# Forget-gate logits: moved from fp32 matmuls at the start to VectorE multiply-and-sum tasks spread over the middle

## The chip, the cores and the metric

The kernel runs on one core of one Trainium2 chip. The metric is the device time of one execution in microseconds (us). Five engines work side by side, each with its own instruction queue in program order: TensorE (PE in the profile, with PEld for its weight loads), VectorE (DVE), ScalarE (ACT), GpSimd (POOL) and SyncE (SP, which here only issues DMAs).

## The reference, cut to what matters

One layer of a gated hybrid encoder, 512 tokens by 2048 channels, all float32. Everything is projected from the normalised input; four columns of that projection are the forget logits, one for each head of branch A:

```python
hn = rmsnorm(x, norm_g)                                  # (1, 512, 2048)
proj = jnp.einsum('bsd,dc->bsc', hn, w_in)               # 6144 + 4 + 6144 columns
f_logit = proj[..., QKVG_COLS:QKVG_COLS + N_HEADS] + b_f # the 4 forget columns
...
log_f = jax.nn.log_sigmoid(f_logit)                      # in forgetting_attention (branch A)
c = jnp.cumsum(log_f, axis=1)
logits = logits + c[:, :, lo:hi, None] - c[:, :, None, :hi]
```

Branch A is attention with this cumulated bias; branch B is attention over a band with a learned bias; branch C is stick-breaking attention. Each branch output is gated, projected up, weighted by merge gates, summed, projected once more and added to x.

The forget logit of a token is therefore rstd[token] times the dot product of its 2048 inputs with w_f * norm_g, for each of four heads, plus b_f.

## The kernel before, in words

**The matmuls.** Weights arrive in float32 tiles of 128 x 1024 (`raw`, eight buffers). ACT rounds each to a high part (`wh`, line 375, three buffers), DVE subtracts to get the low part (`wl`, line 383, two buffers), and PE makes three products of the halves (all through the helper of line 265). One such tile is a *unit*; a list `units` gives the order. The first 9 units are the projection of head 0 of branch C, with x read, scaled and split at the same time; the next 8 are the first block of merge gates; then come 11 stretches of 28 units, each a Strassen product (seven products of half size) that gives one more head and one more block of gates. After them follow the up projections and the output projection. POOL issues DMAs that add a second weight tile onto the first for some Strassen products.

**The order.** A planner (`Flow`) runs when the kernel is built. Every piece of work is a generator that yields what it needs: an event, a number of buffers (`Slots`), or an engine with an estimated duration. The planner takes the piece that can start first on its engine and, among equals, the one that is due first (its ready time plus its `slack`); the instructions are written out in this order, and each engine keeps to it. `fetch` issues a load on SP's queue and estimates its landing. The function `at(u, g, slack)` starts the piece `g` when PE begins unit `u`.

**Buffers.** `t2s` stands for 20 tiles of 128 x 512 float32 in SBUF, shared by all attention work; pieces with a slack over 1 must leave one free. `atts` stands for 4 PSUM banks for attention, `accs` for the 4 banks of the units.

**The forget logits before.** x is kept transposed (channels on partitions). While the first head is projected, `quad(..., early=True)` puts, after the units that end at k tile 11 and 15, eight float32 matmuls each: the 128 x 4 slice `wf` of the constants is stationary, the scaled x tile (`xraw`) streams with 512 columns, and `tile_position` places four of them side by side in the array, so that `first_ps` gets four partial sums. Only then (`f_used`) may `combos` overwrite those x tiles with the sums that Strassen needs. `take_f` copies the bank out and stores it to DRAM; `norm_x` stores rstd to DRAM with one element for each descriptor; `forget_bias` (from unit 17 on) loads both back in another layout, with heads on groups of 32 partitions and 16 tokens in a row, adds the four partial sums, multiplies with rstd, makes the log-sigmoid with small instructions and stores it in `fd2`. The first reader is the softmax of head 0 of branch A (`soft_start`, which broadcasts a row of `fd2` and cumulates it), in the eighth Strassen stretch.

Of the kernel before, what the change touches and what calls it, by code (L numbers as in the profile page):

```python
# [15 lines left out]
P = 128  # L16
# [147 lines left out]
def hybrid_kernel(  # L164
# [2 lines left out]
    xT: bass.AP,  # L167
    xn: bass.AP,
    consts: bass.AP,
    w_col: bass.AP,  # L170
    b_gate: bass.AP,
    rel: bass.AP,
# [36 lines left out]
    def att():  # L209
        return pt.tile([P, S], F32, tag="att", name=nm("att"))  # L210
# [84 lines left out]
    gn = small_in[:, 0:KT]  # L295
    gqk = small_in[:, KT:KT + 4]
    bfc = small_in[:, KT + 4:KT + 5]
    wf = small_in[:, KT + 5:].rearrange("p (k h) -> p k h", h=NH)

    oneb = cp.tile([P, P], BF16, name="oneb")  # L300
    nc.vector.memset(oneb, 1.0)
# [112 lines left out]

    raw_hi = [Event() for _ in range(KT)]
    raw_ev = [Event() for _ in range(KT)]
    scaled, f_used = [Event() for _ in range(KT)], [Event() for _ in range(KT)]
    used_g = [Event() for _ in range(UK)]
    x1 = [Parts("x1", [raw_ev[k], Event()]) for k in range(UK)]
    x2 = [Parts("x2", [raw_ev[k + UK]] * 2) for k in range(UK)]  # L420
# [1 line left out]
    t23 = [None] * UK  # L422
    t4 = [None] * (UK // 2)
    xraw, x_in = [None] * KT, [Event() for _ in range(KT)]
    first_ps = att()
    atts.free.pop()
    nc.vector.memset(first_ps, 0.0)
    early_ps = att()
    for _ in range(WARM):
        nc.tensor.matmul(early_ps[:, :P], oneb, oneb, start=True, stop=True)  # L430
# [49 lines left out]
        yield DVE, dve_us(size)  # L480
        nc.vector.scalar_tensor_tensor(y, w, 1.5, t, op0=ALU.add, op1=ALU.mult)

    rd = dp.tile([QB, P], F32, name="rd")

    def norm_x():

        for i in range(NQ * QB):
            yield n_in[i]
            yield ACT, 0.75, 12.0 + 1.5 * i
            x = xnat[i // 2][:, i % 2, :]  # L490
            nc.scalar.activation(x, x, AF.Square, accum_out=ssq[:, i // NQ, i % NQ:i % NQ + 1])
        give(xps, UK)
        small_n = cp.tile([P, 4, QB], F32, name="small_n")
        m, tmp = small_n[:, 0, :], [small_n[:, i, :] for i in range(1, 4)]
        yield DVE, 0.2
        nc.vector.tensor_reduce(m, ssq, axis=AX.X, op=ALU.add)
        yield from rsqrt(rstd, m, D, tmp, QB)
        set_(rstd_ev)
        nc.sync.dma_start(rd.rearrange("b p -> p b"), rstd)

    def combos(k):

        due = (70.0 + 3 * k,)
        late = (80.0 + 3 * k,)
        for kt in (k, k + UK):
            yield raw_ev[kt]
            yield f_used[kt]
        a, b = xraw[k], xraw[k + UK]
        q = dve_us(HS)
        yield (DVE, q, *due)  # L510
        nc.vector.tensor_sub(a[:, LH], a[:, LH], a[:, RH])
        yield (DVE, q, *due)
        nc.vector.tensor_sub(a[:, RH], b[:, RH], a[:, RH])
        yield (DVE, q, *due)
        minus(b[:, RH], b[:, RH], a[:, LH])
        yield (DVE, q, *due)
        minus(b[:, LH], b[:, RH], b[:, LH])
        yield xps, 1
        t23[k] = Parts("t23")
# [187 lines left out]

    gl = {}
    yd = {}
    f_ev, f2_ev = Event(), Event()  # L710
    fd, fd2 = dp.tile([4, NH, S], F32, name="fd"), dp.tile([NH, S], F32, name="fd2")

    def forget_bias():

        T = S // 32
        lf = cp.tile([P, 5 * T], F32, name="lf")
        v, u, s, p, r = (lf[:, i * T:(i + 1) * T] for i in range(5))
        yield f_ev
        yield rstd_ev
        nc.sync.dma_start(lf[:, :4 * T].rearrange("p (g t) -> p g t", g=4), fd.rearrange("g h (c t) -> (h c) g t", t=T))  # L720
        for h in range(NH):
            nc.sync.dma_start(r[32 * h:32 * (h + 1), :], rd.rearrange("b (c t) -> (b c) t", t=T))
        yield Event(f_ev.t + 8.0)
        q = 0.15
        yield DVE, 4 * q
        nc.vector.tensor_add(v, v, u)
        nc.vector.tensor_add(s, s, p)
        nc.vector.tensor_add(v, v, s)
        nc.vector.tensor_mul(v, v, r)
        yield DVE, 2 * q  # L730
        nc.vector.tensor_scalar(v, v, bfc, 0.0, op0=ALU.add, op1=ALU.add)
        nc.vector.scalar_tensor_tensor(u, v, -1.0, v, op0=ALU.mult, op1=ALU.min)
        yield ACT, q
        nc.scalar.activation(u, u, AF.Exp)

        yield DVE, 5 * q
        nc.vector.tensor_scalar_add(s, u, 2.0)
        nc.vector.reciprocal(s, s)
        nc.vector.tensor_mul(s, s, u)
        nc.vector.tensor_mul(u, s, s)  # L740
        nc.vector.tensor_scalar_mul(p, u, 1.0 / 17.0)
        for k in range(7, 0, -1):
            yield DVE, q
            nc.vector.scalar_tensor_tensor(p, p, 1.0 / (2 * k + 1), u, op0=ALU.add, op1=ALU.mult)
        yield DVE, 4 * q
        nc.vector.scalar_tensor_tensor(p, p, 1.0, s, op0=ALU.add, op1=ALU.mult)
        nc.vector.tensor_scalar_mul(p, p, 2.0)
        nc.vector.tensor_scalar(v, v, -1.0, 0.0, op0=ALU.mult, op1=ALU.max)
        nc.vector.tensor_add(v, v, p)
        nc.sync.dma_start(fd2.rearrange("h (c t) -> (h c) t", t=T), v)  # L750
        f2_ev.t = flow.fin + 3.0
# [340 lines left out]
    def quad(parts, g, done, early=False):  # L1092
# [8 lines left out]
        def mms(kts):  # L1101
            def go(u):
                first, last = kts[0] == 0, kts[-1] == KT - 1
                if not early or last:
                    bank = (accs, acc) if first else None
                    yield from products(u, ps, kts, tbs, block, first, last, bank, done=lambda tb: done(tb, ps[tb]),
                                        outer=first or last)
                    if not early:
                        for kt in kts:
                            if kt < UK:  # L1110
                                set_(used_g[kt])
                else:
# [12 lines left out]
                if early and kts[-1] in (11, 15):  # L1125
                    b = kts[-1] - 3
                    eight = [*range(b - UK, b - UK + 4), *range(b, b + 4)]
                    for kt in eight:
                        yield scaled[kt]
                    yield PE, 2.2  # L1130
                    for kt in eight:
                        j = kt % 4
                        nc.tensor.matmul(first_ps[32 * j:32 * j + NH, :], wf[:, kt, :], xraw[kt],  # L1133
                                         start=kt < 4, stop=kt >= KT - 4, tile_position=(0, 32 * j))
                    for kt in eight:
                        set_(f_used[kt])
            return go

        def src(kts):
# [5 lines left out]
    def take_f():  # L1145
        yield t2s, 1
        yield ACT, act_us(S)
        v = t2("f")
        nc.scalar.activation(v, first_ps, AF.Copy)
        give(atts)  # L1150
        for j in range(4):
            nc.sync.dma_start(fd[j], v[32 * j:32 * j + NH, :])
        stored(t2s, 1, 16)
        f_ev.t = flow.fin + 3.0

    def first_head():
        hd = Head(C, 0)
# [7 lines left out]
        units[-1].after = take_f  # L1165
        u0 = len(units)
        at(u0 - 2, lambda: brow(0))

# [4 lines left out]
            give(accs)  # L1173

        units.extend(quad([[k, k + 1] for k in range(0, KT, 2)], gate_group(0), gates_done))
        at(u0 + OFF["fb"], forget_bias)
        for d, g in hd.stages():
            at(u0 + 1 + 2 * d // 3, g)

# [283 lines left out]
NX = 28  # L1463
NR = 8

OFF = dict(cs=4, ct=12, co=14, s=8, t=14, o=16, s1=3, t1=4, o1=5, fb=8)

_OUT = (QB, NQ, P, S)

# [45 lines left out]
```

## Time and profile before

| what | value |
|---|---|
| median of 3 runs | 1312.24 us (1312.24 to 1312.25) |
| profiled execution | 1312.22 us, of which 1310.5 us span |
| PE busy | 1305.2 us |
| DVE, ACT, POOL busy | 1026.3, 755.6, 91.3 us |
| moved by DMA | 266.03 MB, mean 203 GB/s |
| TensorE clock granted | 1.000 |

The span runs from the first to the last instruction; the execution's time has 1.7 us more around it. The profile groups instructions by line, engine and tile names, gives for each engine what ended its idle times, and follows the chain of work that ended last back to the start. The weight loads (PEld) have measured starts, which makes their distance a good clock for the pace of PE; the ends of matmuls are modelled.

### The profile page before, as it was taken

The page shows a single profiled execution, that of the slowest core. Times are in us where ns is not written, and L with a number is a line of the kernel's source. Part 1 is how long each engine was busy: PE and PEld are TensorE (multiplying, and loading weights), DVE is VectorE, ACT ScalarE, POOL GpSimd, SP SyncE. Part 2 cuts the span into 40 slices and gives each one's busy share as a digit, 9 for nine tenths or more (in the row PEclk, how much of TensorE's full clock was granted, in tenths as well). Part 3 has the DMA queues.
Part 4 walks back from the last instruction along what each step waited for, and adds up shares of the span by engine and source line. Part 5 has one row for each costly group of instructions (what it writes and reads, how often), then busy time and mean ns, then how long its engine had stood idle before and what let it go on. Part 6 is the DMA issues. An engine that isn't in the chain of part 4 may idle for free.

```text
span 1310.5 us, 17137 instructions
## 1 busy us (share of the span) xinstructions
PE 1305.2 (100%) x6028; PEld 1079.2 (82%) x6028; DVE 1026.3 (78%) x1422; ACT 755.6 (58%) x1270; POOL 91.3 (7%) x115
## 2 busy tenths in 40 slices
PE   9999999999999999999999999999999999999998
PEld 7788888888888888888888888888888888888887
DVE  6877796897968768687687886877879668798767
ACT  7655465564556646566475764666668555463442
POOL 0000001100111001101011000110100000000110
PEclk9999999999999999999999999999999999999999
DMA  9755677766777768777687776866786756638983
GB/s 357 223 139 146 179 208 197 220 186 184 209 187 225 199 170 231 173 226 201 179 233 166 211 208 179 248 150 203 215 257 212 273 179 198 181 89 258 253 240 129
DMA packets 89063, 266.03 MB, mean 203 GB/s; under 512 B 11264, under 2 KB 11264, under 8 KB 88976
## 3 DMA queue, kind: packets, MB, share of 16 engines
q1 hardware_dynamic: 71552, 205.94, 46.8%
q0 software_dynamic: 14976, 54.53, 23.3%
q10 hardware_dynamic: 2448, 4.46, 0.9%
q8 instruction: 47, 0.77, 0.3%
q14 instruction: 40, 0.33, 0.1%
HBM read 245.19 MB, written 19.70 MB: 202 GB/s over the span
## 4 chain that ended last, share of the span: by engine, by line
PE 99%; DMA 1%; SPq 0%; ACT 0%; DVE 0%; issue 0%
PE acc L265 92%; PE att L816 1%; PE att L941 1%; PE att L1031 1%; PE att L1030 1%; PE att L261 1%; PE att L262 1%; PE att L260 1%; PE att L1029 1%; PE att L1300 1%; DMA raw<-in_w_col 1%; PE att L1133 0%; SPq L277 0%; PE att L913 0%; ACT wh L375 0%; DVE s L703 0%
## 5 line engine op out<-in xcount | busy, mean ns | idle before, releaser
L375 ACT ACTIVATE wh<-raw 128x1024 fp32r<-128x1024 f32 (+1 forms) x404 | 426.5, 1056 | 389.6 <-PE acc L265 326.7
L383 DVE TENSOR_TENSOR wl<-raw,wh 128x1024 fp32r<-128x1024 f32 (+1 forms) x405 | 493.0, 1219 | 195.1 <-PE acc L265 139.8
L265 PE MATMUL acc<-wh,x 128*128 128x512 f32 x1664 | 434.3, 393 | 0.2
L265 PEld LDWEIGHTS acc<-wh,x 128*128 128x128 f32 x1664 | 307.9, 188 | 64.5 <-ACT wh L375 1.0
L265 PE MATMUL acc<-wh,t 128*128 128x512 f32 x1056 | 271.3, 390 | 0.0
L265 PE MATMUL acc<-wl,x 128*128 128x512 f32 x832 | 231.5, 392 | 0.0
L265 PEld LDWEIGHTS acc<-wh,t 128*128 128x128 f32 x1056 | 197.5, 188 | 40.3
L265 PEld LDWEIGHTS acc<-wl,x 128*128 128x128 f32 x832 | 155.2, 188 | 32.2
L265 PE MATMUL acc<-wl,t 128*128 128x512 f32 x528 | 147.9, 391 | 0.0
L281 POOL DMA_DIRECT2D raw<-in_w_col x88 | 76.1, 864 | 879.0 <-ACT wh L375 143.9
L589 DVE TENSOR_TENSOR raw<-raw,raw 128x1024 f32<-128x1024 f32 x104 | 126.6, 1218 | 0.1
L265 PEld LDWEIGHTS acc<-wl,t 128*128 128x128 f32 x528 | 98.4, 188 | 20.1
L265 PE MATMUL acc<-wh,m 128*128 128x512 f32 x448 | 112.9, 389 | 0.0
L265 PE MATMUL acc<-wh,y 128*128 128x512 f32 x384 | 103.1, 390 | 0.0
L265 PEld LDWEIGHTS acc<-wh,m 128*128 128x128 f32 x448 | 84.1, 188 | 17.4
L265 PEld LDWEIGHTS acc<-wh,y 128*128 128x128 f32 x384 | 71.9, 188 | 15.0
L265 PE MATMUL acc<-wl,m 128*128 128x512 f32 x224 | 62.5, 390 | 0.0
L265 PE MATMUL acc<-wl,y 128*128 128x512 f32 x192 | 59.4, 391 | 0.0
L265 PEld LDWEIGHTS acc<-wl,m 128*128 128x128 f32 x224 | 41.9, 188 | 8.8 <-DVE wl L383 0.2
L265 PEld LDWEIGHTS acc<-wl,y 128*128 128x128 f32 x192 | 35.8, 188 | 7.1
L246 ACT ACTIVATE ah<-att 128x512 fp32r<-128x512 f32 (+3 forms) x48 | 20.9, 436 | 30.3 <-PE att L941 30.3
L1266 DVE TENSOR_TENSOR sg<-acc,sg 128x512 f32<-128x512 f32 x48 | 32.8, 689 | 5.0 <-PE acc L265 2.6
(176 smaller groups left out, 1083.9 us busy)
## 6 DMA issues: line engine op xcount, KB each, us to landing
raw<-in_w_col SPq DMA_DIRECT2D x235, 512.0 KB, 4.7
raw<-in_w_col POOLq DMA_DIRECT2D x88, 512.0 KB, 8.2
raw<-in_w_out SPq DMA_DIRECT2D x40, 512.0 KB, 4.7
raw<-in_w_up SPq DMA_DIRECT2D x24, 512.0 KB, 3.8
sg<-gl SPq DMA_DIRECT2D x48, 256.0 KB, 4.7
raw<-in_w_out POOLq DMA_DIRECT2D x16, 512.0 KB, 5.9
gl<-u SPq DMA_DIRECT2D x22, 256.0 KB, 7.9
gl<-s SPq DMA_DIRECT2D x22, 256.0 KB, 4.6
```

Of the source, the lines that this page charges most:

```text
L246: nc.scalar.activation(hi, src, AF.Copy)
L260: nc.tensor.matmul(ps, lh, rh, start=start, stop=False, skip_group_check=more)
L261: nc.tensor.matmul(ps, lh, rl, start=False, stop=False, skip_group_check=more)
L262: nc.tensor.matmul(ps, ll, rh, start=False, stop=stop, skip_group_check=more)
L265: nc.tensor.matmul(ps, w, x, start=start, stop=stop, skip_group_check=more)
L281: nc.gpsimd.dma_start(to, src, accum_op=ALU.add)
L375: nc.scalar.activation(u.hi, u.raw, AF.Copy)
L383: nc.vector.tensor_sub(u.lo, u.raw, f(u.hi))
L589: nc.vector.tensor_add(to.raw, to.raw, self.raw)
L816: nc.tensor.transpose(ps[:, blk(tb)], self.c[tb][:, blk(r)], identf)
L941: nc.tensor.transpose(ps[:, blk(i)], self.p[i][:, blk(j)], identf)
L1266: nc.vector.tensor_mul(t, ps[tb], t)
```

## The change

The eight plus eight matmuls, `first_ps`, `take_f`, the stores of rstd and of the partial sums, and the waits for `f_used` go. `combos` waits for the scaled x tiles in their place. A new input `wfg` holds the four forget columns and norm_g, both as rows of 128.

- `forget_weights` starts at unit 81: loads `wfg`, multiplies the two on DVE (64 x 128), stores the product `fwd` in DRAM.
- `forget_sums(c, pair)` is started eight times, at units 96, 111, ..., 201, with a slack of 30: for a quarter `c` of the channels and two heads it loads two rows of `fwd`, each broadcast to 128 x 512, and then for each of the four token blocks loads x with tokens on partitions (128 x 512) and runs two fused multiply-and-sum instructions on DVE, one sum for each token and head into `fl`. The product itself is thrown away: for the first head into a PSUM bank, for the second onto x.
- `forget_bias` starts at unit 216: DVE sums the quarters and multiplies with rstd, PE transposes the 128 x 16 result, ACT copies it out, SP stores it and loads it back in the old layout; the small instructions after that are the same, without the four for partial sums and rstd.

```diff
-    first_ps = att()
-    atts.free.pop()
-    nc.vector.memset(first_ps, 0.0)
...
-        nc.sync.dma_start(rd.rearrange("b p -> p b"), rstd)          # norm_x
...
-            yield f_used[kt]                                         # combos
+            yield scaled[kt]
...
+    def forget_weights():
+
+        yield t2s, 1
+        t = t2("fw")
+        yield fetch(t[:NH * KT, :2 * P], wfg, flow.now, 64)
+        yield DVE, 0.25
+        nc.vector.tensor_mul(t[:NH * KT, :P], t[:NH * KT, :P], t[:NH * KT, P:2 * P])
+        nc.sync.dma_start(fwd.rearrange("h (k p) -> (h k) p", p=P), t[:NH * KT, :P])
+        stored(t2s, 1, 32)
+        fw_ev.t = flow.fin + 4.0
+
+    def forget_sums(c, pair):
+
+        yield fw_ev
+        yield t2s, 2
+        hs = range(2 * pair, 2 * pair + 2)
+        ws = [t2("fb") for _ in hs]
+        ev = [fetch(w, fwd[h:h + 1, c * S:(c + 1) * S].to_broadcast([P, S]), flow.now, 256) for w, h in zip(ws, hs)]
+        for tb in range(QB):
+            yield t2s, 1
+            x = t2("xf")
+            yield fetch(x, xn[tb, c], flow.now, 256)
+            yield ev[1]
+            yield atts, 1
+            for w, h, to in zip(ws, hs, (att(), x)):
+                yield DVE, dve_us(S)
+                nc.vector.tensor_tensor_reduce(out=to, in0=x, in1=w, scale=1.0, scalar=0.0, op0=ALU.mult, op1=ALU.add,
+                                               accum_out=fl[:, tb, h, c:c + 1])
+                if to is not x:
+                    give(atts)
+            give(t2s)
+        give(t2s, 2)
+        set_(f_sums[2 * c + pair])
...
     def forget_bias():
...
-        yield f_ev
-        yield rstd_ev
-        nc.sync.dma_start(lf[:, :4 * T].rearrange("p (g t) -> p g t", g=4), fd.rearrange("g h (c t) -> (h c) g t", t=T))
+        for ev in f_sums:
+            yield ev
+        yield DVE, 0.4
+        nc.vector.tensor_reduce(v, fl.rearrange("p b h c -> p (b h) c"), axis=AX.X, op=ALU.add)
+        for b in range(QB):
+            nc.vector.tensor_scalar_mul(v[:, b * NH:(b + 1) * NH], v[:, b * NH:(b + 1) * NH], rstd[:, b:b + 1])
+        yield atts, 1
+        yield PE, 0.11
+        ps = att()
+        nc.tensor.transpose(ps[:T, :P], v, identf)
+        yield t2s, 1
+        yield ACT, 0.3
+        t = t2("ft")
+        nc.scalar.activation(t[:T, :P], ps[:T, :P], AF.Copy)
+        give(atts)
+        nc.sync.dma_start(fd.rearrange("b h p -> (b h) p"), t[:T, :P])
+        stored(t2s, 1, 16)
         for h in range(NH):
-            nc.sync.dma_start(r[32 * h:32 * (h + 1), :], rd.rearrange("b (c t) -> (b c) t", t=T))
-        yield Event(f_ev.t + 8.0)
+            nc.sync.dma_start(v[32 * h:32 * (h + 1), :], fd[:, h, :].rearrange("b (c t) -> b c t", t=T))
+        yield Event(flow.fin + 8.0)
...
-                if early and kts[-1] in (11, 15):                    # quad
-                    b = kts[-1] - 3
-                    eight = [*range(b - UK, b - UK + 4), *range(b, b + 4)]
-                    for kt in eight:
-                        yield scaled[kt]
-                    yield PE, 2.2
-                    for kt in eight:
-                        j = kt % 4
-                        nc.tensor.matmul(first_ps[32 * j:32 * j + NH, :], wf[:, kt, :], xraw[kt],
-                                         start=kt < 4, stop=kt >= KT - 4, tile_position=(0, 32 * j))
-                    for kt in eight:
-                        set_(f_used[kt])
...
-        at(u0 + OFF["fb"], forget_bias)
+        at(u0 + 8 + FAT, forget_weights, 30.0)
+        for r in range(8):
+            at(u0 + 8 + FAT + FGAP * (r + 1), lambda r=r: forget_sums(r // 2, r % 2), 30.0)
+        at(u0 + 8 + FAT + FGAP * 9, forget_bias)
...
+FAT, FGAP = 64, 15
```

Here `u0` is 9. The constants that are loaded first shrink from 85 to 21 float32 columns.

More of the change, by code (lines that the diff above doesn't have):

```diff
@@ L169, in hybrid_kernel @@
     consts: bass.AP,
+    wfg: bass.AP,
     w_col: bass.AP,
@@ L297, in hybrid_kernel @@
     bfc = small_in[:, KT + 4:KT + 5]
-    wf = small_in[:, KT + 5:].rearrange("p (k h) -> p k h", h=NH)
     oneb = cp.tile([P, P], BF16, name="oneb")
@@ L416, in hybrid_kernel @@
     raw_ev = [Event() for _ in range(KT)]
-    scaled, f_used = [Event() for _ in range(KT)], [Event() for _ in range(KT)]
+    scaled = [Event() for _ in range(KT)]
     used_g = [Event() for _ in range(UK)]
@@ L481, in rsqrt @@
         nc.vector.scalar_tensor_tensor(y, w, 1.5, t, op0=ALU.add, op1=ALU.mult)
-    rd = dp.tile([QB, P], F32, name="rd")
     def norm_x():
@@ L709, in hybrid_kernel @@
     yd = {}
-    f_ev, f2_ev = Event(), Event()
-    fd, fd2 = dp.tile([4, NH, S], F32, name="fd"), dp.tile([NH, S], F32, name="fd2")
+    f2_ev, fw_ev = Event(), Event()
+    f_sums = [Event() for _ in range(8)]
+    fd, fd2 = dp.tile([QB, NH, P], F32, name="fd"), dp.tile([NH, S], F32, name="fd2")
+    fwd = dp.tile([NH, D], F32, name="fwd")
+    fl = cp.tile([P, QB, NH, NQ], F32, name="fl")
+    def forget_weights():
[28 more added lines that the diff above has]
+        set_(f_sums[2 * c + pair])
     def forget_bias():
@@ L717, in forget_bias @@
         v, u, s, p, r = (lf[:, i * T:(i + 1) * T] for i in range(5))
-        yield f_ev
-        yield rstd_ev
-        nc.sync.dma_start(lf[:, :4 * T].rearrange("p (g t) -> p g t", g=4), fd.rearrange("g h (c t) -> (h c) g t", t=T))
+        for ev in f_sums:
[15 more added lines that the diff above has]
+        stored(t2s, 1, 16)
         for h in range(NH):
-            nc.sync.dma_start(r[32 * h:32 * (h + 1), :], rd.rearrange("b (c t) -> (b c) t", t=T))
-        yield Event(f_ev.t + 8.0)
+            nc.sync.dma_start(v[32 * h:32 * (h + 1), :], fd[:, h, :].rearrange("b (c t) -> b c t", t=T))
+        yield Event(flow.fin + 8.0)
         q = 0.15
[L725 to L729, printed above, removed]
         yield DVE, 2 * q
@@ L1143, in quad @@
         return [Unit(mms(k), shape=(len(k), S), srcs=[src(k)]) for k in parts]
[L1145 to L1154, printed above, removed]
     def first_head():
@@ L1164, in first_head @@
         units.extend(quad([[0], [1]] + [[k, k + 1] for k in range(2, KT, 2)], group(C, 0), done, True))
-        units[-1].after = take_f
         u0 = len(units)
@@ L1464 @@
 NR = 8
-OFF = dict(cs=4, ct=12, co=14, s=8, t=14, o=16, s1=3, t1=4, o1=5, fb=8)
+OFF = dict(cs=4, ct=12, co=14, s=8, t=14, o=16, s1=3, t1=4, o1=5)
+FAT, FGAP = 64, 15
 _OUT = (QB, NQ, P, S)
@@ L1487 @@
     bf = np.repeat(g["b_f"][0], P // NH).reshape(P, 1)
-    consts = [g["norm_g"][0].reshape(KT, P).T, g["qk_norm_g"][0].T, bf,
-              w[:, nq:nq + NH].reshape(KT, P, NH).transpose(1, 0, 2).reshape(P, KT * NH)]
+    consts = [g["norm_g"][0].reshape(KT, P).T, g["qk_norm_g"][0].T, bf]
     rel = g["rel_bias"][0]
@@ L1497 @@
         "consts": np.concatenate(consts, axis=1),
+        "wfg": np.concatenate([w[:, nq:nq + NH].T.reshape(NH * KT, P), np.tile(g["norm_g"][0].reshape(KT, P), (NH, 1))],
+                              axis=1),
         "w_col": w_col,
```

## The prediction

> **What bounds the kernel now.** I read the page's busy shares first, then the chain that ended last, then what PE's weight loads waited for after the start, then whom the two splitting engines wait for.
>
> ```profile
> span 1310.5 us, 17137 instructions
> PE 1305.2 (100%) x6028; PEld 1079.2 (82%) x6028; DVE 1026.3 (78%) x1422; ACT 755.6 (58%) x1270; POOL 91.3 (7%) x115
> PE 99%; DMA 1%; SPq 0%; ACT 0%; DVE 0%; issue 0%
> ...
> PEld L913 <- issue: 1.7, 8, 0.3
> PEld acc L265 <- DVE wl L383: 0.2, 1, 0.2
> ...
> ACT wh L375 <- PE acc L265: 326.7, 205, 5.7
> DVE wl L383 <- PE acc L265: 139.8, 125, 2.4
> ```
>
> The chain is PE for 99%. The two PEld rows are the whole list of waits from 60 us to the end: in 1250 us PE waited once, 0.2 us, for another engine. The last two rows say that ACT and DVE wait for PE to free the weight buffers, so they run ahead of it. Each microsecond of PE work taken out is one of the time, and work put on DVE costs nothing until it makes a split late.
>
> **What the change removes.** The first row is the chain's entry for one of the two groups of forget matmuls; the others are starts of PE's weight loads around both.
>
> ```profile
> 39.48 1.83 PE att L1133 x16
> ...
> 26.07 1.77 PEld L265 LDWEIGHTS acc<-wl,x 128*128 128x128 f32 x8
> 31.51 1.77 PEld L265 LDWEIGHTS acc<-wl,x 128*128 128x128 f32 x8
> 37.29 1.77 PEld L265 LDWEIGHTS acc<-wl,x 128*128 128x128 f32 x8
> 41.24 3.50 PEld L265 LDWEIGHTS acc<-wh,x 128*128 128x128 f32 x16 [0.86 <-ACT x L463]
> 44.78 1.77 PEld L265 LDWEIGHTS acc<-wl,x 128*128 128x128 f32 x8
> ...
> 49.31 0.87 PEld L265 LDWEIGHTS acc<-wh,x 128*128 128x128 f32 x4
> 50.67 0.87 PEld L265 LDWEIGHTS acc<-wh,x 128*128 128x128 f32 x4
> ...
> 55.45 0.87 PEld L265 LDWEIGHTS acc<-wh,x 128*128 128x128 f32 x4
> ```
>
> By the chain a group costs 1.83 us, two 3.66. But pace tells more. Undisturbed, wl loads follow each other at 31.51 - 26.07 = 5.44 us; across the first group it is 44.78 - 37.29 = 7.49, so it cost 2.05. In the second place the pitch is 50.67 - 49.31 = 1.36; across the group two pitches (2.72) became 55.45 - 50.67 = 4.78, so it cost 2.06. I take **4.11 us**. The 0.86 us of idle at 41.24 that is put down to ACT belongs to it: the load ahead of the next matmuls does not overlap these.
>
> The Trainium skill, page "TensorEngine Tiling (Array Packing)", section "Key Properties", says that a change of tiling mode drains TensorE. That speaks for the pitch (4.11) against the chain's entry (3.66), since the group has its own mode; by the chain alone the forecast would be 0.45 us later.
>
> **Does PE get the 4.11, or wait for its data instead?** The start is dense:
>
> ```profile
> 20.00:40.00 20.00, 19.96 (x93) 15.63 (x95) 12.15 (x18) 18.75 (x39) 0.00 (x0) 1.00 1.04 397
> ...
> 34.67 2.35 PEld L265 LDWEIGHTS acc<-wh,x 128*128 128x128 f32 x11 [0.47 <-ACT x L246]
> 35.14 1.04 ACT L375 ACTIVATE wh<-raw 128x1024 fp32r<-128x1024 f32 x1
> 37.36 1.35 DVE L250 TENSOR_TENSOR x<-x,x 128x512 fp32r<-128x512 f32 x2
> ```
>
> From 20 to 40 us ACT is 94% busy, the DMA share is 1.04, and PE waited 0.47 us for an x tile at 34.67. Without the first group the next unit's loads begin at 37.29 + 1.81 (eight loads; 5.44 us hold 24) = 39.10. Its weights were split by ACT at 36.18, its last low x part ended at 38.71, and the low parts come eight matmuls (1.8 us) into the unit. So all of it is there 0.4 us before the unit begins, and the low parts 2.2 us before their use. `combos` may now start before 41 us, and a `t` split could slip ahead of an x split on ACT; it has a much later due time, so at most one short instruction (0.4 us) at a time. I take 0 and keep 0 to 0.8. If none of the first group's gain were kept, 2.05 of the 4.11 would go.
>
> Other removals off the path: the bank's memset, `take_f`, its stores, small instructions, and this wait, during which SP issued no weights:
>
> ```profile
> SPq L722 <- DMA rd<-rstd: 9.5, 1, 9.5
> ```
>
> It hid behind weight tiles loaded ahead; nothing is gained on PE.
>
> **What it adds on PE.** One 128 x 128 transpose in place of 16 matmuls.
>
> ```profile
> 60.82 0.44 PE att L816 x4
> ```
>
> 0.44 / 4 = 0.11 us; alone it may lose some overlap; I take 0.14. It waits for a reduce and four small multiplies on DVE, which the planner counts 0.4 us. One such instruction took 0.15 (below), so five take about 0.75, and with the planner's 0.12 and 0.25 of margin PE waits 0 to 0.4: I take **0.2**.
>
> **What it adds on DVE.** 8 tasks x 4 token blocks x 2 heads = 64 fused instructions of 128 x 512. The nearest rows are the same instruction in a branch B softmax (PSUM in, SBUF out), a write to PSUM by DVE, and DVE's load where the tasks lie:
>
> ```profile
> 442.26 0.69 DVE L917 CUSTOM_DVE_ANT_0 p<-att,tb 128x512 f32<-128x512 f32 x1
> 442.87 0.08 DVE L917 DVE_READ_ACCUMULATOR2_ANT mx<- 128x1 f32 x1
> 442.99 0.15 DVE L919 TENSOR_SCALAR mx<-mx 128x1 f32<-128x1 f32 x1
> ...
> 1.18 0.48 DVE L427 MEMSET att<- 128x512 f32 x1
> ...
> 300.00:640.00 340.00, 340.00 (x1570) 282.48 (x1569) 263.88 (x351) 200.99 (x344) 27.62 (x32) 1.00 0.73 199
> 347.70:358.00 10.30, 10.30 (x47) 8.55 (x46) 10.27 (x16) 6.54 (x9) 0.00 (x0) 1.00 0.48 152
> ```
>
> From its start to the next instruction it took 442.99 - 442.26 = 0.73 us; the memset has no input and bounds a PSUM output from below (0.48), the pair's summed durations from above (0.77). 64 x 0.73 = **47 us**. The planner counts 0.64 each, 0.09 less.
>
> Where: two Strassen stretches are 82.66 us apart, 28 units of 2.95 us.
>
> ```profile
> 213.49 31.34 PE acc L265 x138
> ...
> 296.15 31.34 PE acc L265 x138
> ```
>
> The loads above give unit 17 at about 98 us (54.2 + 8 x 5.44), hence the tasks at about 331 us and every 44 us to 642. In 300 to 640 us DVE is idle for 340 - 264 = 76 us, 47 of which are taken; DVE goes from 78 to about 91%. Some 10 us stretches are full already (10.27 of 10.30), but there PE does not wait today, and a fused instruction is due 30 us after its x, behind splits (2.5) and attention (5): it can hold a split up by one instruction, 0.73 us. In plan, that is free. Its cover is the lead of the splits over PE, priced below.
>
> **What it adds on the queues.** Each task loads 2 + 4 tiles of 256 KB, 1.57 MB; 12.6 MB in all.
>
> ```profile
> q1 hardware_dynamic: 71552, 205.94, 46.8%
> ...
> 420.10:430.40 10.30, 10.30 (x49) 8.53 (x48) 7.88 (x13) 5.43 (x9) 1.72 (x2) 1.00 1.05 314
> ```
>
> SP's queue moved 205.94 MB in 46.8% of 1310.5 us, 336 GB/s, so a task takes 4.7 us of DMA time. That fits on average (share 0.73, plus 8 x 4.7 of 340 = 0.84), but where stretches begin the engines are full (1.05). There weights and other loads come late already:
>
> ```profile
> tb<-in_rel SPq DMA_DIRECT2D x4, 256.0 KB, 11.9
> DVE tb L896 <- DMA tb<-in_rel: 1.9, 3, 0.9
> ...
> 434.84 1.06 ACT L375 ACTIVATE wh<-raw 128x1024 fp32r<-128x1024 f32 x1 [3.97 <-DMA raw<-in_w_col]
> 439.21 0.87 PEld L265 LDWEIGHTS acc<-wh,x 128*128 128x128 f32 x4
> ```
>
> The split at 434.84 waited 4.0 us for its tile, ended at 435.90, and its unit's loads began at 439.21: 3.3 us were left. A task beginning at about 420 us puts two rows and one x tile (0.8 MB, 2.3 us) ahead of this; 1.0 us is left. DVE waited at most 0.9 us for a `tb` tile that took 11.9 us, and PE did not notice. I take 0 for both, keeping 0 to 5 us.
>
> The end of the chain of forget logits is not tight: `forget_bias` starts at about 331 + 8 x 44 = 683 us; earlier its small instructions took from 103.3 to 114.8, and with 8 us for its loads and a few for DMA it ends by about 712. The first row is wanted at 752.4:
>
> ```profile
> L726 DVE TENSOR_TENSOR lf<-lf x1: 167/167/167, 103.3 to 103.3; 128x16 f32<-128x16 f32 x1
> L750 SPq DMA_DIRECT2D fd<-lf x1: 319/319/319, 114.8 to 114.8; - x1
> L277 SPq DMA_DIRECT2D cr<-fd x4: 424/456/482, 752.4 to 977.6; - x4
> ```
>
> Held buffers (three of 20 tiles, one PSUM bank) can delay attention, but not PE, whose units go on without it.
>
> **Sum.** - 4.11 + 0.14 + 0.2 = - 3.77 us. The profiled execution took 1312.22 us (1310.5 span), 0.02 under the median of the runs shown: 1312.22 - 3.77 = 1308.45, said as **1308.5 us**, 0.29% faster.
>
> **The rivals.**
> (1) *Waits in DVE's queue give part of it back.* Each of 32 x tiles is waited for by a fused instruction with splits and attention results queued behind it. If a tile lands like `tb` (0.9 us late) on top of one interposed instruction (0.73), that is 1.6 us; where it meets a lead of 1.2 to 1.4 us (1.0 was left above), PE waits 0.2 to 0.4 us per task, 1.6 to 3.2 in all: 1310.0 to 1311.7, no change that can be measured. For it: full stretches. Against: the three late `tb` tiles cost PE nothing. The Trainium skill ("TensorE: Matmul & The Clock Gate", section on engine queue depths) calls VectorE a strict FIFO, which is why a wait there reaches what is behind it; no row here shows it reach PE.
> (2) *The start does not give it.* PE would wait for x tiles or weights in the first group's place: 4.11 - 2.05 - 0.34 = 1.7 us gained, 1310.5. For: ACT at 94%, 0.47 us waited. Against: the ends at 36.18 and 38.71.
> (3) *Slower: weights come late where stretches begin.* If all 4.7 us of a task fall ahead of a tile with 3.3 us of lead, PE waits 1.4 us; over eight tasks 11, and 1312.2 - 3.8 + 11 = 1319.6. It decides from 0.47 us per task (3.77 / 8), a delay of 3.8 us. For: the share of 1.05 and the 4.0 us wait. Against: only three tasks (331, 420, 508 us) fall on such a place, and only half of a task's loads go out at once; three alone would cost 4.2, 1312.7. The page "DMA: Bandwidth & Descriptors" of the Trainium skill, section "Anatomy of one DMA", reckons 436 GB/s for the movement; by that a task takes 3.6 us (an estimate) and the lead nearly covers it. The 336 and 314 GB/s here are lower, so the rows speak more for this rival than the page.
>
> **How the numbers follow.** Forecast 0.60 (1308.1 to 1309.5: the transpose free at best, 0.8 at the start and 0.2 more at the transpose at worst). Rival 1: 0.18; rival 2: 0.08; rival 3: 0.13, a third of it with three tasks only, near no change; 0.01 for better. A measurement here can tell about 0.2% (2.6 us). Faster by more than that: 0.61; within: 0.29; slower: 0.10. The range 1307.8 to 1313.0 (0.3 below the best case for the reading of the pitches) takes in all but the strong form of rival 3, about 1 in 10.
>
> **What would show it.** Right: no L1133 rows, the wl loads after 37.29 come 5.44 us later, the first Strassen stretch begins 4.1 us earlier and all that follows keeps that shift through 331 to 690 us; PEld waits there stay under 1 us; DVE's busy time rises by about 49 us. Wrong: PEld waits for `wl` or `wh` between 331 and 690 us (rivals 1 and 3 are told apart by whether DVE waited for `xf` tiles or ACT for `raw`), or at 39 to 42 us for x (rival 2).

## The result: 3.0 us faster, and the profile after

The changed kernel took 1309.27 us (median of 11 runs, 1308.31 to 1310.45) against 1312.25 us (11 runs) on the same chip. The ratio is 0.9977 with a 95% interval of 0.9969 to 0.9984, so the change gains 2.98 us or 0.23%, where 3.77 were forecast. The profiled execution is the median one: 1309.27 us, span 1307.6.

The page of the changed kernel, and from its lists the two forms of the fused instruction, the landing time of the x tiles and the stretch of the tasks (columns as before):

```profile
span 1307.6 us, 17293 instructions
PE 1300.9 (99%) x5997; PEld 1077.4 (82%) x5997; DVE 1059.2 (81%) x1551; ACT 753.5 (58%) x1270; POOL 91.3 (7%) x115
...
q1 hardware_dynamic: 77520, 218.53, 49.3%
...
xf<-in_xn SPq DMA_DIRECT2D x32, 256.0 KB, 6.9
...
L736 DVE CUSTOM_DVE_ANT_0 att<-xf,fb x32: 665/694/702, 338.6 to 685.5; 128x512 f32<-128x512 f32 x32
L736 DVE CUSTOM_DVE_ANT_0 xf<-xf,fb x32: 623/684/693, 340.4 to 691.6; 128x512 f32<-128x512 f32 x32
...
300.00:640.00 340.00, 339.27 (x1564) 281.07 (x1564) 291.77 (x461) 199.03 (x343) 27.62 (x32) 1.00 0.81 232
```

PE is still the bound, but from 300 to 640 us it now has 0.73 us of gaps that it did not have. The queue moved 12.6 MB more, as reckoned. The product may go to PSUM or onto x at the same price (694 and 684 ns).

The starts of PE's weight loads, where the matmuls were:

```profile
30.67 1.77 PEld L266 LDWEIGHTS acc<-wl,x 128*128 128x128 f32 x8
...
34.17 2.59 PEld L266 LDWEIGHTS acc<-wh,x 128*128 128x128 f32 x12 [0.51 <-ACT x L247]
36.80 1.77 PEld L266 LDWEIGHTS acc<-wl,x 128*128 128x128 f32 x8
...
42.24 1.77 PEld L266 LDWEIGHTS acc<-wl,x 128*128 128x128 f32 x8
...
50.85 0.87 PEld L266 LDWEIGHTS acc<-wh,x 128*128 128x128 f32 x4
...
52.21 0.87 PEld L266 LDWEIGHTS acc<-wh,x 128*128 128x128 f32 x4
```

42.24 - 36.80 is 5.44, and 52.21 - 50.85 is 1.36, the undisturbed distances: both groups are gone from the pace, and nothing took their place.

All that PE waited for from 60 us on, and what DVE waited for from DMAs between 300 and 720 us (us in total, times, longest):

```profile
PEld acc L266 <- DVE wl L383: 2.1, 5, 1.1
PEld L953 <- issue: 1.7, 8, 0.3
PEld att L758 <- DVE lf L754: 1.0, 1, 1.0
```

```profile
DVE att L736 <- DMA xf<-in_xn: 9.1, 5, 3.9
DVE tb L936 <- DMA tb<-in_rel: 7.3, 3, 2.7
DVE lf L771 <- DMA lf<-fd: 2.7, 1, 2.7
```

Before, the first list held 0.2 us for `wl`. Now DVE stands 9.1 us before x tiles that have not landed, 7.3 (from 1.9) before `tb` tiles, and PE waits for DVE. The longest case, from SP's, DVE's and PEld's orders in time:

```profile
464.56 0.92 SPq L278 DMA_DIRECT2D xf<-in_xn  x2
...
471.46 0.70 DVE L736 CUSTOM_DVE_ANT_0 att<-xf,fb 128x512 f32<-128x512 f32 x1 [3.86 <-DMA xf<-in_xn]
...
472.08 1.22 DVE L383 TENSOR_TENSOR wl<-raw,wh 128x1024 fp32r<-128x1024 f32 x1
...
473.36 0.30 PEld L266 LDWEIGHTS acc<-wl,t 128*128 128x128 f32 x2 [1.15 <-DVE wl L383]
```

Two x loads are issued from 464.56 us. DVE reaches the first fused instruction at 467.6, waits 3.86 us, and the split behind it starts 0.62 us later still, at 472.08. PE waits 1.15 us for that split.

What the change is worth along the way is the start of a unit before minus that of the same unit after. The columns are times in the kernel before. The first lies ahead of the matmuls. I take it as scatter of the start, since the ten kernels with the change's start spread from -0.22 to 0.50 there; a few tenths from the smaller constants are not ruled out. All kernels of the section below are in the table:

| kernel | 33 us | 54 | 330 | 409 | 515 | 681 | 719 | 1303 | median of runs, us | ratio to before (95%) |
|---|---|---|---|---|---|---|---|---|---|---|
| the change | 0.50 | 4.68 | 4.62 | 4.62 | 3.36 | 3.39 | 2.60 | 2.61 | 1309.27 | 0.9977 (0.9969 to 0.9984) |
| e1: before, without the matmuls | -0.27 | 3.89 | 3.81 | 3.81 | 3.81 | 3.81 | 3.81 | 3.79 | 1307.99 | 0.9966 (0.9952 to 0.9979) |
| e2: no loads, no sums | 0.16 | 4.32 | 4.25 | 4.25 | 4.26 | 4.25 | 4.13 | 4.11 | 1307.77 | 0.9964 (0.9951 to 0.9976) |
| e3: loads, no sums | 0.01 | 4.20 | 4.14 | 1.14 | 1.13 | 1.12 | 1.01 | 0.98 | 1311.14 | 0.9992 (0.9983 to 1.0000) |
| e4: sums, no loads | 0.37 | 4.54 | 4.47 | 4.45 | 4.45 | 4.48 | 2.65 | 1.91 | 1309.84 | 0.9979 (0.9970 to 0.9988) |
| e5: x landing +2.5 us | 0.34 | 4.52 | 4.45 | 4.45 | 4.46 | 4.08 | 3.99 | 4.00 | 1308.04 | 0.9970 (0.9959 to 0.9982) |
| e6: bias estimates | 0.09 | 4.27 | 4.21 | 4.21 | 4.23 | 3.53 | 3.45 | 3.42 | 1309.29 | 0.9976 (0.9968 to 0.9985) |
| e7: both, and room | -0.22 | 3.95 | 3.89 | 3.88 | 3.81 | 3.77 | 3.63 | 3.59 | 1308.84 | 0.9975 (0.9965 to 0.9985) |
| e8: e7 at other places | 0.44 | 4.62 | 4.55 | 2.47 | 2.47 | 1.93 | 2.26 | 2.25 | 1309.88 | 0.9983 (0.9975 to 0.9992) |
| e9: x landing -2.5 us | 0.28 | 4.45 | 4.39 | 0.31 | -4.92 | -7.09 | -14.33 | -14.36 | 1326.42 | 1.0115 (1.0097 to 1.0133) |
| e10: e5 and e6 together | 0.32 | 4.50 | 4.43 | 4.43 | 4.46 | 2.89 | 2.81 | 2.77 | 1308.86 | 0.9970 (0.9958 to 0.9982) |

The change's row reads: 4.18 us from the two groups, nothing to speak of lost to 409 us, 1.26 lost by 515 (0.2 with two short waits of PE at 443 and 448 us of the changed kernel, 1.0 with the one at 473), 0.79 lost where the logits are finished, then nothing. With 0.50 at the start and a tail 0.3 us shorter that is 2.9, the difference of the spans. The tail belongs to the change: from DVE's last arithmetic to the end of the span it is 3.31 us in the kernel before and in e1, and 2.96 or 2.97 in nine of the ten kernels with the change (3.18 in e8). Why is not known.

### The profile page after: what moved, and what is told of

Read it like the earlier page. It is cut to its first block, busy times and chain, and to the rows that moved or that the text cites. A ratio compares the mean times of both kernels' runs of the same rounds, so it can differ in the third digit from the quotient of the medians.

```text
span 1307.6 us, 17293 instructions
## 1 busy us (share of the span) xinstructions
PE 1300.9 (99%) x5997; PEld 1077.4 (82%) x5997; DVE 1059.2 (81%) x1551; ACT 753.5 (58%) x1270; POOL 91.3 (7%) x115
## 3 DMA queue, kind: packets, MB, share of 16 engines
q10 hardware_dynamic: 2448, 4.46, 0.9%
## 4 chain that ended last, share of the span: by engine, by line
PE 96%; DMA 2%; DVE 1%; ACT 0%; SPq 0%; issue 0%; DVEq 0%; ACTq 0%
PE acc L266 90%; DMA x<-in_xT 1%; PE att L856 1%; PE att L981 1%; PE att L1071 1%; PE att L1070 1%; PE att L262 1%; PE att L263 1%; PE att L261 1%; PE att L1069 1%; PE att L1319 1%; DMA xf<-in_xn 1%; DMA xn<-in_xn 0%; DVE wl L383 0%; DVE x L251 0%
## 5 line engine op out<-in xcount | busy, mean ns | idle before, releaser
L266 PEld LDWEIGHTS acc<-wl,x 128*128 128x128 f32 x832 | 155.1, 188 | 32.9 <-DVE wl L383 0.7
L1285 DVE TENSOR_TENSOR sg<-acc,sg 128x512 f32<-128x512 f32 x48 | 32.9, 690 | 5.0 <-PE acc L266 2.6
```

The source lines that it names most:

```text
L266: nc.tensor.matmul(ps, w, x, start=start, stop=stop, skip_group_check=more)
L1285: nc.vector.tensor_mul(t, ps[tb], t)
```

## The experiments

### What are the matmuls worth, and what does the rest cost? (e1, e2)

e1 is the kernel before without the sixteen matmuls (its forget sums are the zeros of the bank); everything around them stays.

```diff
-                    yield PE, 2.2
-                    for kt in eight:
-                        j = kt % 4
-                        nc.tensor.matmul(first_ps[32 * j:32 * j + NH, :], wf[:, kt, :], xraw[kt], ...)
```

> The kernel before, without the sixteen forget matmuls (the bank keeps its zeros, so the forget logits are b_f alone); all the rest, the large constants and the early forget chain included, stays. My theory: the matmuls cost 4.1 us by the pitch of the weight loads, and PE gets all of it: 1308.1 us (4.1 less), with the shift of 2.05 at each of the two places and the same from there to the end. Rival (the chain's entry): 3.7 less. Rival (part of the changed kernel's start, 4.6 us ahead at unit 9, comes from the smaller constants): then this one is 4.1 ahead at unit 9 and not 4.6.

e2 is the changed kernel without the loads and sums of the eight tasks (`fl` holds a constant); the transpose and the way through DRAM stay.

```diff
+    nc.gpsimd.memset(fl, 0.01)
...
         yield fw_ev                                      # forget_sums: all between here
-        ...
         set_(f_sums[2 * c + pair])                       # and here
```

> The changed kernel without the sums: no loads of x and of the weight rows, no fused instructions (the sums are a constant); forget_weights and the later forget_bias with its transpose stay. My theory: of the changed kernel's loss after the start, about 1.2 us lie where DVE waited for x tiles (440 to 476 us) and 0.8 us at the transpose and the loads behind it, so this runs 1.2 us faster than the changed kernel: 1308.0, with a shift of 4.6 us up to 690 us and 3.8 after. Rival (the sums are free, the loss is the transpose and chance alone): 1309.2.

e1 gained 4.16 us between its first two columns and kept 4.08 of it from 330 us on. e2 gained the same and lost 0.14 where the logits are finished. Its whole list of PE's waits from 60 us on:

```profile
PEld L936 <- issue: 1.7, 8, 0.3
PEld acc L266 <- DVE wl L383: 0.4, 2, 0.2
```

So the matmuls are worth 4.1 to 4.2 us, by pitch and not by the chain's 3.66; and the loads and sums together cost about 1.5 us (1309.27 - 1307.77), where I had reckoned nothing. The rival about the smaller constants stays open: e1, with the large ones, is 3.89 ahead at 54 us, below all kernels with the small ones (3.95 to 4.68), but by less than those differ among themselves.

### Loads or instructions? (e3, e4)

e3 keeps the loads and drops the sums (`fl` is a constant); a tile is held until 2 us after the time at which it is reckoned to land. e4 keeps the 64 fused instructions, but on one tile that a memset fills, with no load.

```diff
-            for w, h, to in zip(ws, hs, (att(), x)):     # e3
-                yield DVE, dve_us(S)
-                nc.vector.tensor_tensor_reduce(out=to, in0=x, in1=w, ...)
+            yield Event(flow.ready + 2.0)
+            t2s.free += [there.t + 2.0]
```

```diff
-        ws = [t2("fb") for _ in hs]                      # e4
+        fx = t2("fb")
+        nc.vector.memset(fx, 1.0)
         for tb in range(QB):
-            yield fetch(x, xn[tb, c], flow.now, 256)
-            yield ev[1]
+            yield Event(flow.now + 4.0)
```

> The changed kernel with all 48 loads of the sums but without the 64 fused instructions, so nobody waits for the loads. If the loss comes from DVE standing before a tile that has not landed (my theory), it goes: 1308.0, no PE wait between 331 and 690 us. If it comes from DMA being crowded so that weights land late (rival), it stays: 1309 or more, with PE waits for wh or wl around 430 to 480 us.

> The changed kernel with the 64 fused instructions on DVE (and 8 memsets) but on a tile that is in SBUF already, no loads; tiles held are one in place of three for each task. If the 47 us of DVE work itself pushes splits late (rival), the loss stays: 1309 or more. If only the landing matters (my theory): 1308.0 to 1308.3, no PE wait for wl over 0.3 us before the transpose.

e4's sums cost nothing: 4.47 at 330 us and 4.48 at 681, and PE had no wait for `wl` between. Its time still missed the 1308.0 to 1308.3, since it lost 2.6 us afterwards, where the logits are finished. PE waited 0.61 us before the transpose, 1.24 us behind the reload and once more, 0.90 us, at 718.59. Below are SP's wait for the store, DVE's for the reload and PE's for DVE:

```profile
SPq L764 <- DMA fd<-ft: 5.9, 1, 5.9
...
709.70 0.23 DVE L768 TENSOR_SCALAR lf<-lf,small_in 128x16 f32<-128x16 f32 x1 [3.91 <-DMA lf<-fd]
...
711.47 0.30 PEld L266 LDWEIGHTS acc<-wl,t 128*128 128x128 f32 x2 [1.24 <-DVE wl L383]
```

e3 missed altogether: 1308.0 and no wait of PE were expected, and it lost 3.0 us between 330 and 409 with no fused instruction on DVE at all. Windows of e2 and then of e3 (us, busy time of PE, PEld, DVE, ACT and POOL, clock, DMA share, GB/s), and e3's waits of PE, DVE and ACT there:

```profile
340.00:350.00 10.00, 10.00 (x45) 8.26 (x44) 9.70 (x17) 6.44 (x11) 0.00 (x0) 1.00 0.89 292
350.00:360.00 10.00, 10.00 (x46) 8.27 (x45) 9.96 (x11) 7.87 (x12) 0.00 (x0) 1.00 0.17 54
```

```profile
340.00:350.00 10.00, 9.84 (x44) 7.78 (x42) 5.06 (x10) 5.08 (x12) 0.86 (x1) 1.00 1.05 344
350.00:360.00 10.00, 9.11 (x40) 7.48 (x41) 10.00 (x17) 6.72 (x11) 0.00 (x0) 1.00 0.25 95
...
PEld acc L266 <- DVE wl L383: 3.4, 4, 1.5
...
DVE vl L888 <- DMA gl<-u: 1.7, 1, 1.7
...
336.10 0.28 ACT L1007 ACTIVATE p<-att 128x128 f32<-128x128 f32 x1 [2.95 <-DMA fb<-fwd]
```

With the loads the DMA engines are full at 340 to 350 us, attention gets tiles late, DVE does half of what it did there (5.06 against 9.70 us), and at 350 it has that work and the next to do at once. The splits are late, and PE waits.

Two kinds of late tiles stand in the rows. DVE waits for tiles whose old contents are still being stored (`gl<-u`). And ahead of that ACT waits 2.95 us for a tile into which a row of `fwd` is still being loaded (`fb<-fwd`). That second wait is e3's own: nothing reads its loads, so the planner hands a tile on 2 us after its reckoned landing, and the next writer has to wait for the real one. In the changed kernel neither ACT nor attention's work on DVE waits for `fb` or `xf`, and it loses nothing at this place. So e3 does not price the loads of the change. It shows a second way to PE: attention that gets its tiles late piles up on DVE ahead of the splits. What e4 settles is that the cost is not DVE's busy time. Whether it is x tiles that come late into an order already written is tested next.

### Is it the place of the wait in DVE's order? (e5, e9)

The order is written with the planner's landing times. e5 and e9 change one number, the time at which an x tile is reckoned to be there; no instruction is added or removed.

```diff
-            yield fetch(x, xn[tb, c], flow.now, 256)
-            yield ev[1]
+            there = fetch(x, xn[tb, c], flow.now, 256)
+            yield Event(max(there.t, ev[1].t) + 2.5)     # e5;  - 2.5 in e9
```

> The changed kernel with one number changed: the planner reckons each x tile of the sums 2.5 us later (and its fused instructions accordingly). In the changed kernel's profile PE fell back 1.2 us between 440 and 476 us, where DVE stood 3.9 and 3.0 us before x tiles that had not landed. If that landing is the cause (my theory), the DVE waits for xf shrink to about 1.5 us each and PE keeps its 4.6 us of lead up to 690 us: 1308.2, 1.0 under the changed kernel. If the tight tile pool is the cause (rival, the loads alone cost 3.1 us because tiles that are held make attention and its DVE work bunch up), it doesn't help, or hurts, since tiles are held longer: 1309.3 or more.

> The changed kernel, but the planner reckons each x tile to land 2.5 us sooner than it did (the other direction from the run with 2.5 us added, which took 1308.04 us against 1309.27). Theory (DVE is put before x tiles that aren't there, and what stands behind it in its order comes late): the waits of DVE at L736 for xf grow from 5 (9.1 us) to more than 15 (over 30 us), PE's waits for wl between 300 and 720 us from some 2 us to 4 to 10, and the time rises to between 1310.5 and 1316 us. Rival (the 1.2 us that the later reckoning brought were run-to-run scatter, or came from another order of the tasks): DVE waits longer for xf, but PE's waits for wl stay within 1 us of the changed kernel's, and the time stays at 1308.5 to 1310.

e5's waits of PE for `wl` and of DVE for x tiles, and the order of DVE where PE lost 1.15 us in the changed kernel:

```profile
PEld acc L266 <- DVE wl L383: 0.4, 2, 0.2
...
DVE att L736 <- DMA xf<-in_xn: 1.6, 2, 1.1
...
469.01 1.23 DVE L383 TENSOR_TENSOR wl<-raw,wh 128x1024 fp32r<-128x1024 f32 x1 [0.88 <-issue]
470.15 0.69 DVE L736 CUSTOM_DVE_ANT_0 att<-xf,fb 128x512 f32<-128x512 f32 x1
```

The split now stands ahead of the fused instruction, the tile has landed when DVE comes to it, the waits for x fall from 9.1 to 1.6 us, and PE keeps 4.46 us to 515 us. (It loses 0.4 later, with a wait of 0.59 us for attention's DVE work at 534.5 us.) e9's same two lists, and the worst of its places:

```profile
PEld acc L266 <- DVE wl L383: 14.9, 13, 4.6
...
DVE att L736 <- DMA xf<-in_xn: 26.1, 12, 5.7
...
678.73 0.48 SPq L278 DMA_DIRECT2D xf<-in_xn  x1
...
689.84 0.70 DVE L736 CUSTOM_DVE_ANT_0 att<-xf,fb 128x512 f32<-128x512 f32 x1 [5.73 <-DMA xf<-in_xn]
...
692.93 1.22 DVE L383 TENSOR_TENSOR wl<-raw,wh 128x1024 fp32r<-128x1024 f32 x1
...
694.20 1.35 PEld L266 LDWEIGHTS acc<-wl,x 128*128 128x128 f32 x4 [4.58 <-DVE wl L383]
```

DVE waited 5.73 us for a tile, six more rows of DVE stand between it and the split, and PE waited 4.58 us. The theory named the sign and the mechanism, though DVE's waits for x grew to 12 (26.1 us) and not to over 15 (30 us). The size was far beyond what I expected (1326.42 against 1310.5 to 1316), for two reasons: PE waited 14.9 us for `wl` and not 4 to 10, and after long waits its clock fell, as windows at two places show:

```profile
433.00:437.00 4.00, 2.23 (x11) 1.52 (x10) 4.00 (x8) 1.04 (x2) 0.00 (x0) 1.00 1.05 417
437.00:441.00 4.00, 4.00 (x16) 3.63 (x15) 3.93 (x11) 0.33 (x2) 0.00 (x0) 0.57 0.50 185
...
688.00:694.00 6.00, 2.05 (x10) 1.35 (x8) 4.16 (x8) 1.06 (x1) 0.00 (x0) 0.94 0.66 260
694.00:697.00 3.00, 2.79 (x7) 2.22 (x8) 2.96 (x7) 1.06 (x1) 0.00 (x0) 0.50 0.23 88
697.00:700.00 3.00, 3.00 (x12) 2.83 (x11) 2.91 (x11) 1.00 (x4) 0.00 (x0) 0.50 0.02 5
```

If half the clock means half the pace, 6 us of it cost about 3.0 (an estimate), and with the wait of 4.58 that is 7.6; the row of e9 falls by 7.24 between 681 and 719 us. One number in an estimate, moved 2.5 us either way, is thus worth 1.2 us one way and 17 the other.

### The finish of the logits, and the places of the tasks (e6, e7, e8, e10)

e6 reckons 1.5 us for the reduce and multiplies ahead of the transpose and 14 us for the way through DRAM, somewhat more than the changed kernel's trace shows (0.87 and 11.0). e7 adds 4 us to each x tile and starts a task only with seven tiles free, a load only with four. e8 is e7 with the tasks at units 11 and 17 of four stretches, away from the stretches' beginnings, and with `forget_weights` and `forget_bias` moved to match. e10 is e5 and e6 together.

```diff
-        yield DVE, 0.4                                   # e6, e7, e8, e10: forget_bias
+        yield DVE, 1.5
-        yield Event(flow.fin + 8.0)
+        yield Event(flow.fin + 14.0)
+        yield lambda: len(t2s.free) >= 7                 # e7, e8: ahead of a task's rows
+            yield lambda: len(t2s.free) >= 4             #   and of each x tile
-            at(u0 + 8 + FAT + FGAP * (r + 1), ...)       # e8
+            at(u0 + 8 + 28 * (2 + r // 2) + (11, 17)[r % 2], ...)
```

> The changed kernel with two estimates of forget_bias changed: 1.5 us in place of 0.4 for the five DVE instructions ahead of the transpose, 14 us in place of 8 for the way through DRAM. In the profile PE waited 1.0 us before the transpose and DVE 2.7 us before the reloaded logits; PE fell back 0.8 us between 694 and 710 us. My theory: the estimates are the cause, so the 0.8 come down to 0.15 and DVE's wait for lf vanishes: 1308.6. Rival (the last sums crowd DVE there whatever the estimate): no change, 1309.3.

> Both, and a room for tiles: x is reckoned 4 us later, a task starts only with 7 of the 20 tiles free and takes a further x tile only with 4 free, and the two estimates of forget_bias are mended. If late landings, the tight pool and the estimates are all of the loss (my theory): 1307.8, as the kernel without sums, with PE keeping 4.3 us or more from 54 us to the end. If the 47 us of DVE work cost something that no order avoids (rival): 1308.5 or more.

> As the kernel with both estimates and room for tiles, with the eight tasks put where stretches are quiet (units 11 and 17 of four stretches) and forget_bias at unit 13 of the sixth. My theory: DMA share there is 0.5 to 0.7 and DVE 6.4 to 7.1 of 10.3 us, so no x tile is late and nothing is lost: 1307.8, equal to the one without places chosen. Rival: two tasks within 6 units hold six tiles together and attention is delayed: 1308.5 or more.

> The changed kernel with both estimates mended: x tiles reckoned 2.5 us later, the reduce and four multiplies ahead of the transpose 1.5 us in place of 0.4, the loads of the logits 14 us in place of 8 after the store. Theory: the later landing keeps what is left by 640 us at 3.9 to 4.5 us, and the bias then costs 0.1 to 0.2, so 1307.7 to 1308.4 us, the fastest of the versions with the change. Rival (what is left of the cost depends on how the order happens to fall at the crowded places, not on these estimates): a loss of 0.6 us or more at one of the stretch beginnings, and 1308.6 to 1309.6.

e6 lost 0.1 us at the logits' finish instead of 0.79, but its median did not move, since it lost 0.7 near 540 us. e7 held everything from 54 us to the end within 0.4 us; its median is 0.4 under the change's, and its profiled run had begun 0.7 us worse. That median, 1308.84, lies where its rival was put (1308.5 or more: a cost that no order avoids); the profile, in which PE has no wait for DVE beyond e2's, does not bear the rival out, but nothing excludes it. e8 was the miss: my quiet places were not quiet. It lost 2.1 us by 409 us, in four waits of PE between 352 and 367 us. No x tile was late there. ACT's and PEld's orders show what was:

```profile
342.27 0.51 ACT L892 ACTIVATE vh<-w 128x128 fp32r<-128x128 f32 x2 [4.59 <-DMA gl<-u]
...
352.59 0.76 PEld L266 LDWEIGHTS acc<-wl,x 128*128 128x128 f32 x4 [0.89 <-DVE wl L383]
```

ACT stood 4.59 us for a tile whose old contents were still being stored, attention's work piled up on DVE, and the splits came late, as in e3. That fits e8's rival (tasks that hold tiles delay attention), but no run separates the held tiles from a full queue. DVE's longer waits in e8, 10.8 us for four `tb` tiles from 434 us on, were followed by no wait of PE for `wl`.

e10 was expected to be the fastest and was not. Up to the transpose near 695 us its order is the same as e5's, instruction by instruction, and still it had lost 1.6 us by 681 where e5 lost 0.4. The first `tb` tile of that stretch in e5 and then in e10:

```profile
513.75 0.11 DVE L936 MEMSET tb<- 64x64 f32 x1 [2.75 <-PE acc L266]
```

```profile
514.96 0.11 DVE L936 MEMSET tb<- 64x64 f32 x1 [3.93 <-DMA tb<-in_rel]
```

In one run the tile was there; in the other DVE stood 3.93 us for it, and PE waited 2.3 us for DVE, in five pieces, between 516 and 536 us. The change and e6 likewise share one order up to there, and lost at 445 to 473 us in the one profile and near 540 in the other. The order says where a late tile can hurt; whether it comes late differs from run to run. So the runs of equal orders belong together: 12 of e5 and e10 have a median of 1308.24 us, 23 of the change and e6 1309.27 (medians of the kernel before beside them: 1312.16 to 1312.26). The later landing is worth about 1.0 us (1.2 by e5 alone). That is a rough size, since the two groups overlap: 1307.40 to 1310.64 us with it, 1307.58 to 1311.18 without.

By its median e5 is the fastest version that computes everything: 1308.04 us, ratio 0.9970 (0.9959 to 0.9982). Its lead over e10 (1308.86) is within the scatter.

## Why the prediction was nearly right

- **The matmuls, 4.11 us:** right (4.18 here, 4.16 in e1), and so was the choice of the pitch over the chain's 3.66. The Trainium skill, "TensorEngine Tiling (Array Packing)", section "Key Properties", says that a change of tiling mode drains TensorE. The 0.22 us that each group cost beyond its 1.83 fit that, but no run here separates such a drain from other lost overlap.
- **The start (rival 2):** nothing was lost; the weight loads follow at 5.44 and 1.36 us.
- **64 fused instructions, 0.73 us each, free in plan:** right, by e4. They follow each other at 0.62 us where DVE is dense. My check that DVE's busy time would rise by 49 us was wrong; it rose by 32.9. Busy time counts overlapping instructions once; summed one by one, DVE's durations rose by 52.
- **The waits that the new loads bring into DVE's order, 0 in the sum ("I take 0 for both, keeping 0 to 5 us"): the step that failed.** They cost about 1.2 us, at the small end of that bound. This is rival 1 in part (price 1.6 to 3.2): DVE standing before x tiles with splits behind, which is also the prediction's own sign of being wrong (PE's waits for `wl` came to 1.7 us between 442 and 474). I had sized the lateness by the three late `tb` tiles (0.9 us); x tiles took 6.9 us to land and DVE stood up to 3.9 us for one. The Trainium skill, "TensorE: Matmul & The Clock Gate", section "Architectural detail: the array is 16× 32×32, not 1× 128×128", in its lines on engine queue depths, calls VectorE a strict FIFO; the wait of 3.86 us passed on to PE at 473 us agrees.
- **Rival 3 (weights late by the queue):** not seen at PE. Between 300 and 720 us ACT stood 17.7 us for weight tiles, 9.9 in the kernel before, but from 60 us on PE waited for `wl`, never for `wh`, and in e5 and e7, which load the same, for almost nothing. (The rival's 1319.6 holds with 1.4 us for each of eight tasks, 11.2 and not 11.)
- **The transpose, 0.14 + 0.2: mis-sized.** The finish cost 0.79. These rows are of DVE, PEld and SP:

```profile
695.65 0.21 DVE L752 TENSOR_REDUCE lf<-fl 128x16 f32<-128x64 f32 x1
695.90 0.62 DVE L754 TENSOR_SCALAR lf<-lf,rstd 128x4 f32<-128x4 f32 x4
...
696.57 0.09 PEld L758 LDWEIGHTS att<-identf,lf 128*16 128x16 f32 x1 [0.97 <-DVE lf L754]
...
697.18 0.34 SPq L764 DMA_DIRECT2D fd<-ft  x1
...
702.66 3.07 SPq L767 DMA_DIRECT2D lf<-fd  x4
...
708.15 0.23 DVE L771 TENSOR_SCALAR lf<-lf,small_in 128x16 f32<-128x16 f32 x1 [2.74 <-DMA lf<-fd]
```

  The five small instructions took 0.87 us from first start to last end, near my 0.75, but DVE reached them late and PE stood 0.97 us. And I had priced no wait at all on the reload: DVE stood 2.74 us for it. With the same instructions and no sums the finish cost 0.14 (e2), and with the two estimates mended 0.1 (e6).
- **"Held buffers can delay attention, but not PE": wrong in its second half.** In e3 and e8 attention that got its tiles late piled up on DVE, and PE lost 3.0 and 2.1 us; how much of that the held buffers made is open. In the change itself it did not show.
- **The sum:** 1308.45 was 0.8 us early; 1309.27 lies in the likeliest case's own range (1308.1 to 1309.5). That is partly luck. The range left room for 0.8 at the start, where nothing was lost, and 0.2 more at the transpose. What was lost was 1.26 and 0.79 elsewhere, which alone would leave about 2.1 of the 4.1; in the profile a start that lay 0.50 us ahead and a tail 0.3 us shorter, neither of them forecast, brought it back to 2.9.

Three things stay open: why a load of one and the same order lands some us later in one run than in another, whether held tiles or the full queue make attention's tiles late in e3 and e8, and what shortens the tail. None was tried.

## What to carry to other kernels

Work put on an idle engine may cost nothing in busy time and still cost through its waits: look at what stands behind each wait in that engine's order, and price it by how late its tile can land, not by how long the instruction is. Where a planner writes the order, reckoning a landing too late was cheap here and too early was dear (1.2 us gained against 17 lost for 2.5 us either way), so set landing times by the slow end of what the trace shows. And a matmul group was worth its pitch, the distance that the loads around it lose, not its entry in the chain.

## What the runs showed that I had not expected

- A wait of PE costs twice when it is long. After 4.58 us without work the granted clock was 0.50 for 6 us, and after 2.19 us (436.17 us in e9) it was 0.57 over the next 4 us; after 1.15 us in the changed kernel and 1.48 us in e3 it stayed at 1.00. The Trainium skill, "TensorE: Matmul & The Clock Gate", Part 1, puts the idle window at about 3.4 us; here a wait shorter than that was enough.
- A 256 KB tile took 6.9 us to land (median), and in e9 one took from 678.73 or 679.84 to 689.84, some 10 us, while the DMA share was 1.04.
- The logits' way through DRAM took 11.0 us in the changed kernel (697.18 to 708.15) and 12.6 in e4 (697.13 to 709.70), 5.9 of them SP's wait for an 8 KB store, where the planner reckoned 8.
